# Two block pairs by seven products, and convolution taps moved from VectorE to ScalarE, in a two-layer encoder trunk

## The chip, the cores and the metric

The kernel runs on one core of a Trainium2 chip. The metric is the device time in microseconds (us) of one execution; lower is better. Everything is float32; matrix products use the `float32r` type in a scheme with split operands that is described below.

The engines, with the names of the profile: PE is the matrix engine TensorE (PEld its weight loads), DVE is VectorE, ACT is ScalarE, POOL is GpSimd, SP is the engine that issues most weight loads. Each engine works through its own queue in order, and waits at the head of the queue for semaphores of the others.

## The reference, cut to what matters

Two layers. Each has an attention part (neither changed nor described further here) and a gated feed-forward part with a convolution over positions, width 3:

```
h2 = rms_norm(x, ln2_g[l])                               # (256, 2048)
u  = depthwise_conv(h2 @ w_up[l], conv_w[l], conv_b[l])  # (256, 11264): 3 taps and a bias per column
gate, up = u[..., :5632], u[..., 5632:]
x  = x + (silu(gate) * up) @ w_down[l]                   # back to (256, 2048)
```

## The kernel before

**Tiles.** 256 tokens are two halves of 128 rows. The inner width of 5632 is 44 tiles of 128 (`f` = 0 to 43). The 2048 output columns are four blocks of 512 (`nb` = 0 to 3), and blocks 0 and 1, and blocks 2 and 3, are the two pairs that the change speaks of.

**Split operands.** Every operand of a large product is split into a high part (a copy rounded to `float32r`, written by ACT, `whi` for weights) and the rest (input minus high part, written by DVE, `wlo`). A product is then three: high by high, high by rest, rest by high. The split is in `split` (L114 on ACT, L115 on DVE). So every 1024 columns of weights that PE uses cost one ACT and one DVE instruction of 128x1024 first.

**Quanta and steps.** The work of a layer is a list, `quanta`: each quantum has one weight block of 1 MB (`raw`, three buffers) and a body. A quantum is two or three steps of 1024 weight columns; four steps ahead of PE (`SPLIT_AHEAD`) the split of a step is issued, into five rotating `whi` and five `wlo` buffers. So the high part of a step can only be written once PE is through with the step five before it. Four kinds of quantum matter; the letters are used in the rest of the document:

- U (`q_up`): half of the up projection of one tile `f`; two of them make a tile, which from here on is called one U: 4 steps, 64 products. At its end comes `glu`: add the two parts out of PSUM (`prob`, L548 on ACT and L549 on DVE), scale (`halo`, L550), copy the edge columns (POOL), apply the three taps (L558 on ACT for the middle one; L560 on DVE for the neighbours, two taps by two halves), gate, multiply, split into `mid` tiles. After each odd `f`, `sums_mid` makes four sums for S.
- D (`q_down`): one output block by four tiles of `f`: 2 steps, 24 products with 512 columns.
- S (`q_seven`): a pair of output blocks by two tiles of `f`, by seven products where eight are usual (two token halves, two blocks, two tiles). 6 of the 7 are in S: 3 steps, 18 products of 512 columns. Before the second step DVE forms sums of the weights in `raw` (L755, L756, L757). S over four tile pairs sums up in PSUM; then `add_seven` adds the seven results into `x` (seven additions on DVE, one copy on ACT).
- P (`q_plain`): the seventh product for the eight tiles of a portion: 2 steps, 12 products, and one addition into `x` (L657).

A layer has five portions of `f`: four of 8 tiles and one of 12 (`CHUNKS`). In the first four, blocks 0 and 1 go through S and P, blocks 2 and 3 through D. The order of a portion in steady state: eight U, then P, then S D S D S D S D. The first portion has nine U ahead, so that U is always one tile early.

**Low parts by transfer.** The last step of each U gets its rest not from DVE but from an accumulating DMA (L775 on ACT writes minus the high part into `v_a` or `v_b`, L776 on POOL issues the transfer that adds `raw`).

**What sets the order.** The Tile framework schedules the instructions of each engine ahead of time, by priorities and a model of the times; the queues on the chip then run in that order. `high_priority` around splits moves them forward.

Of the kernel before, what the change touches and what calls it, by code (L numbers as in the profile page):

```python
# [31 lines left out]
NF = FF // P  # L32
# [5 lines left out]
PART = 8  # L38
# [16 lines left out]

SPARE = 3 * (("qT", 3),)

# [4 lines left out]
def encoder_kernel(  # L62
# [107 lines left out]
    def stat_o(grp):  # L170
        ps = psum.tile([P, TT], F32, name="pv", bufs=1)
        for tt in range(TT):
            mm(ps[:, tt:tt + 1], acc_o[grp][:, tt * P:(tt + 1) * P], ones[:, 0:1], True, True)
        st["ro"] = act.tile([P, 16], F32, name="ro", bufs=2)[:, 0:TT]
        rsqrt(ps, 1.0 / (NH * HD), st["ro"], "c2")
# [92 lines left out]
    def evac_qk(ps, nh, kind):  # L268

        n = nh * HD  # L270
        grp, isq = kind[1], kind[0] == "q"
# [246 lines left out]
    gs = {}  # L518
    count = {}

    def middle(l, f):

        name, bufs = "mid", MIDS
        if f >= NF - CHUNKS[-1]:
            k = count[l] = count.get(l, 0) + 1
            if k > MIDS:
                name, bufs = SPARE[k - MIDS - 1]
        return act.tile([P, 2, T], F32R, name=name, bufs=bufs)

# [14 lines left out]
    def glu(l, f, ps):  # L544
# [8 lines left out]
        nc.gpsimd.tensor_copy(ux[:, :, T + r:T + 2 * r - 1], ux[:, :, r + 1:2 * r])  # L553
        y = work.tile([P, 2, T], F32, name="pT", bufs=4)
        for j in range(2):
            c = j * NF + f
            w0, w1, w2, b = (par["conv"][:, l, i, c:c + 1] for i in range(4))
            nc.scalar.activation(y[:, j, :], ux[:, j, r:r + T], AF.Identity, scale=w1, bias=b)  # L558
            for w, o in ((w0, 0), (w2, 2 * r)):
                nc.vector.scalar_tensor_tensor(y[:, j, :], ux[:, j, o:o + T], w, y[:, j, :],  # L560
                                               op0=ALU.mult, op1=ALU.add)
        nc.scalar.activation(t[:, 0, :], y[:, 0, :], AF.Silu)
# [23 lines left out]

    def q_seven(l, c, i):

# [4 lines left out]
        def body(q, part, hi, lo):  # L593
# [20 lines left out]
    def add_seven(ps):  # L614

        t = work.tile([P, 4, HD], F32, name="tq", bufs=2).rearrange("p a d -> p (a d)")
        x11, x12 = x[:, 0, 0:512], x[:, 0, 512:1024]
        x21, x_2, x2_ = x[:, 1, 0:512], x[:, :, 512:1024], x[:, 1, 0:1024].rearrange("p (j n) -> p j n", j=2)
# [22 lines left out]

    def q_plain(l, c):

        f0 = sum(CHUNKS[:c])

        def body(q, half, hi, lo):
# [8 lines left out]
            if half == 1:  # L655
                xv = x[:, 0, 0:512]
                nc.vector.tensor_add(xv, xv, ps)  # L657
        return body

# [42 lines left out]
    for l in range(L):  # L702
# [8 lines left out]
        for c, nf in enumerate(CHUNKS):  # L711
            up = lambda f: [(a["w_up"][l, f, u], q_up(l, f, u), "up") for u in range(2)]
            down = lambda nb, g: [(a["w_down"][l, sum(CHUNKS[:c]) // FG + g, nb], q_down(l, c, nb, g), "")]
            seven = lambda i: [(a["w_seven"][l, c, i], q_seven(l, c, i), "seven")]

            end = sum(CHUNKS[:c]) + PART + 1
            while f < end:
                quanta += up(f)
                f += 1
            quanta.append((a["w_plain"][l, c], q_plain(l, c), ""))  # L720
            if nf == PART:
                for i in range(PAIRS):
                    quanta += seven(i) + down(2 + i // 2, i % 2)
            else:

                for i in range(PAIRS):
# [36 lines left out]
    def by_transfer(s):  # L763
        q, half = steps[s]
        return quanta[q][2] == "up" and half == 1 and last_up[q]

    def low_w(s):

        if s < len(steps) and by_transfer(s):
            q, half = steps[s]  # L770
            src = raw[q][:, half * 1024:(half + 1) * 1024]
            lo = lows[s] = act.tile([P, 1024], F32R, name=("v_a", "v_b")[turns[0] % 2], bufs=1)
            turns[0] += 1
# [137 lines left out]
def _layout(inputs):  # L911
# [33 lines left out]

    four = wd[:, :n * PART * P, :1024].reshape(L, n, PART // 2, 2, P, 2, 512)
    o["w_seven"] = c(np.stack([four[:, :, :, k, :, m] for k, m in ((1, 0), (1, 1), (0, 1), (0, 0))], 4)).reshape(
        L, n, PART // 2, P, 2048)
    o["w_plain"] = c(four[:, :, :, 1, :, 0].transpose(0, 1, 3, 2, 4)).reshape(L, n, P, 2048)
    o["w_down"] = c(f["w_down"].reshape(L, NF // FG, FG, P, NB, 512).transpose(0, 1, 4, 3, 2, 5)).reshape(  # L950
# [40 lines left out]
```

## Time and profile before

| | |
|---|---|
| median of 3 runs | 2098.43 us (2096.87 to 2099.15) |
| the profiled execution | 2098.86 us, span of its instructions 2097.1 us |
| PE busy | 2086.1 us (99%) |
| DVE busy | 1623.0 us (77%) |
| ACT busy | 1308.8 us (62%) |
| POOL busy | 241.5 us (12%) |
| period of one steady portion (8 U, P, 4 S, 4 D) | 129.6 us |
| DVE busy in one such portion | 108.7 us |

A layer is about half of the span; its four portions of eight tiles are eight equal periods in all. The profile's `L` numbers are lines of the kernel before. In the changed kernel the same statements stand some lines lower: `prob` L558, `halo` L559, the multiply by the gate L574, the sums of tiles L587 to L590, the sums of weights L775 to L777, the addition of P L671.

### The profile page before, as it was taken

The page shows a single profiled execution, that of the slowest core. Times are in us where ns is not written, and L with a number is a line of the kernel's source. Part 1 is how long each engine was busy: PE and PEld are TensorE (multiplying, and loading weights), DVE is VectorE, ACT ScalarE, POOL GpSimd, SP SyncE. Part 2 cuts the span into 40 slices and gives each one's busy share as a digit, 9 for nine tenths or more (in the row PEclk, how much of TensorE's full clock was granted, in tenths as well). Part 3 has the DMA queues.
Part 4 walks back from the last instruction along what each step waited for, and adds up shares of the span by engine and source line. Part 5 has one row for each costly group of instructions (what it writes and reads, how often), then busy time and mean ns, then how long its engine had stood idle before and what let it go on. Part 6 is the DMA issues. An engine that isn't in the chain of part 4 may idle for free.

```text
span 2097.1 us, 29473 instructions
## 1 busy us (share of the span) xinstructions
PE 2086.1 (99%) x10816; PEld 1787.8 (85%) x10816; DVE 1623.0 (77%) x2516; ACT 1308.8 (62%) x1905; POOL 241.5 (12%) x325
## 2 busy tenths in 40 slices
PE   9999999999999999999999999999999999999999
PEld 8888888888888888888888888888888888888887
DVE  7786656797887978788857766667978879788786
ACT  7566556766666666576555665567666666666663
POOL 0011101101101011020000111011011110111100
PEclk9999999999999999999999999999999999999999
DMA  9544557858678586787555455578686785867864
GB/s 351 196 145 166 175 181 213 242 204 252 206 253 267 206 258 201 229 272 230 208 181 181 161 169 171 165 220 248 209 256 206 243 254 210 270 199 240 262 211 161
DMA packets 74817, 454.57 MB, mean 217 GB/s; under 512 B 8752, under 2 KB 11312, under 8 KB 26416
## 3 DMA queue, kind: packets, MB, share of 16 engines
q1 hardware_dynamic: 61280, 405.46, 54.4%
q0 software_dynamic: 12672, 46.14, 12.3%
q8 instruction: 85, 1.39, 0.3%
q10 hardware_dynamic: 720, 1.08, 0.2%
q14 instruction: 60, 0.49, 0.1%
HBM read 404.42 MB, written 2.10 MB: 194 GB/s over the span
## 4 chain that ended last, share of the span: by engine, by line
PE 95%; DVE 2%; DMA 1%; issue 1%; ACT 1%; ACTq 0%; DVEq 0%; SPq 0%
PE mm L100 86%; PE S L100 3%; PE pv L100 2%; PE tr L100 1%; DVE wlo L115 1%; PE tr L375 1%; ACT whi L114 1%; PE tr L309 1%; PE S L151 0%; DMA v_a<-raw 0%; DMA mid<-in_xT 0%; DMA raw<-in_w_seven 0%; DMA raw<-in_w_up 0%; DVE pT L560 0%; DVE prob L549 0%
## 5 line engine op out<-in xcount | busy, mean ns | idle before, releaser
L115 DVE TENSOR_TENSOR wlo<-raw,whi 128x1024 fp32r<-128x1024 f32 (+1 forms) x709 | 858.2, 1221 | 298.2 <-ACT whi L114 265.8
L114 ACT ACTIVATE whi<-raw 128x1024 fp32r<-128x1024 f32 (+1 forms) x709 | 736.4, 1053 | 449.9 <-PE mm L100 220.7
L100 PE MATMUL mm<-xs,whi 128*128 128x512 f32 x2816 | 977.0, 390 | 3.0 <-DVE prob L549 3.0
L100 PEld LDWEIGHTS mm<-xs,whi 128*128 128x128 f32 x2816 | 527.8, 188 | 113.9 <-DVE prob L549 3.9
L100 PE MATMUL mm<-xs,wlo 128*128 128x256 f32 x2112 | 596.4, 282 | 0.6 <-DVE wlo L115 0.6
L100 PEld LDWEIGHTS mm<-xs,wlo 128*128 128x128 f32 x2112 | 399.1, 189 | 2.6 <-DVE wlo L115 1.5
L100 PE MATMUL mm<-whi,mid 128*128 128x512 f32 x1412 | 369.9, 392 | 1.6 <-DVE prob L549 1.2
L100 PEld LDWEIGHTS mm<-whi,mid 128*128 128x128 f32 x1412 | 262.5, 188 | 56.6 <-DVE prob L549 2.1
L100 PE MATMUL mm<-whi,xs 128*128 128x512 f32 x1152 | 294.7, 393 | 0.4 <-ACT whi L114 0.4
L100 PEld LDWEIGHTS mm<-whi,xs 128*128 128x128 f32 x1152 | 212.7, 188 | 43.1 <-ACT whi L114 1.4
L100 PE MATMUL mm<-wlo,mid 128*128 128x512 f32 x706 | 201.9, 392 | 0.0
L100 PE MATMUL mm<-wlo,xs 128*128 128x512 f32 x576 | 158.8, 392 | 0.0
L100 PEld LDWEIGHTS mm<-wlo,mid 128*128 128x128 f32 x706 | 132.2, 188 | 27.4
L560 DVE SCALAR_TENSOR_TENSOR pT<-halo,conv,pT 128x256 f32<-128x256 f32 x352 | 148.7, 481 | 6.5 <-ACT pT L558 1.6
L100 PEld LDWEIGHTS mm<-wlo,xs 128*128 128x128 f32 x576 | 107.0, 188 | 21.5
L552 POOL COPY halo<-halo 128x6 f32<-128x6 f32 x88 | 78.4, 891 | 352.8 <-DVE halo L550 352.8
L788 ACT ACTIVATE whi<-raw 128x1024 fp32r<-128x1024 f32 x88 | 92.7, 1053 | 40.1 <-PE mm L100 40.1
L558 ACT ACTIVATE pT<-halo,conv 128x256 f32<-128x256 f32 x176 | 96.0, 592 | 23.2 <-DVE halo L550 21.1
L100 PE MATMUL mm<-xs,v_a 128*128 128x256 f32 x352 | 99.3, 282 | 0.0
L100 PE MATMUL mm<-xs,v_b 128*128 128x256 f32 x352 | 99.2, 282 | 0.0
L776 POOL DMA_DIRECT2D v_b<-raw x44 | 38.1, 866 | 524.1 <-ACT v_b L775 299.6
L549 DVE TENSOR_TENSOR prob<-prob,mm 128x512 f32<-128x512 f32 x88 | 60.3, 685 | 46.9 <-ACT prob L548 46.9
(189 smaller groups left out, 1922.5 us busy)
## 6 DMA issues: line engine op xcount, KB each, us to landing
raw<-in_w_up SPq DMA_DIRECT2D x176, 1024.0 KB, 5.7
raw<-in_w_in SPq DMA_DIRECT2D x71, 1024.0 KB, 4.9
raw<-in_w_down SPq DMA_DIRECT2D x48, 1024.0 KB, 4.9
raw<-in_w_seven SPq DMA_DIRECT2D x40, 1024.0 KB, 5.1
raw<-in_w_out SPq DMA_DIRECT2D x32, 1024.0 KB, 4.8
v_a<-raw POOLq DMA_DIRECT2D x44, 512.0 KB, 5.5
v_b<-raw POOLq DMA_DIRECT2D x44, 512.0 KB, 5.1
raw<-in_w_plain SPq DMA_DIRECT2D x10, 1024.0 KB, 4.9
```

What stands on the lines that cost most here:

```text
L100: nc.tensor.matmul(ps, lhsT, rhs, start=start, stop=stop, skip_group_check=True)
L114: high = nc.scalar.activation(hi, src, AF.Copy)
L115: nc.vector.tensor_sub(lo, src, hi.bitcast(F32))
L309: nc.tensor.transpose(ps[:, j, tt * P:(tt + 1) * P], qn[tt][:, p + j, :], ident)
L375: nc.tensor.transpose(ps[:, kt, tt * P:(tt + 1) * P], p[:, tt, kt * P:(kt + 1) * P], ident)
L549: nc.vector.tensor_add(t, t, ps[:, :, 1])
L552: nc.gpsimd.tensor_copy(ux[:, :, 1:r], ux[:, :, T:T + r - 1])
L558: nc.scalar.activation(y[:, j, :], ux[:, j, r:r + T], AF.Identity, scale=w1, bias=b)
L560: nc.vector.scalar_tensor_tensor(y[:, j, :], ux[:, j, o:o + T], w, y[:, j, :], op0=ALU.mult, op1=ALU.add)
L776: nc.gpsimd.dma_start(out=lo, in_=src, accum_op=ALU.add)
L788: highs[s] = nc.scalar.activation(hl[s][0], raw[q][:, half * 1024:(half + 1) * 1024], AF.Copy)
```

## The change

Four edits.

1. In the first four portions, blocks 2 and 3 go through S and P too (`m` = 1), with their own weights; their D is gone. `add_seven` and P's addition run twice per portion.
2. The order of a portion is now, for each `m`: S, P, S, U, S, U, S, U, U.
3. In `glu` ACT multiplies the neighbour taps (four instructions of 128x256 into two more `pT` tiles) and DVE adds the tiles (two instructions of 128x512), where DVE had four multiply-adds of 128x256.
4. The second step of P gets its rest by transfer, like the last step of U. The tiles for `mid` come from a list of five names with a count of free buffers, since they are kept longer; three tiles change their size by some bytes.

```diff
-        y = work.tile([P, 2, T], F32, name="pT", bufs=4)
+        y, *sides = (work.tile([P, 2, T], F32, name="pT", bufs=4) for _ in range(3))
         for j in range(2):
             ...
             nc.scalar.activation(y[:, j, :], ux[:, j, r:r + T], AF.Identity, scale=w1, bias=b)
-            for w, o in ((w0, 0), (w2, 2 * r)):
-                nc.vector.scalar_tensor_tensor(y[:, j, :], ux[:, j, o:o + T], w, y[:, j, :],
-                                               op0=ALU.mult, op1=ALU.add)
+            for n, w, o in ((sides[0], w0, 0), (sides[1], w2, 2 * r)):
+                nc.scalar.activation(n[:, j, :], ux[:, j, o:o + T], AF.Copy, scale=w)
+        for n in sides:
+            nc.vector.tensor_add(y, y, n)
...
-            if i == PAIRS - 1 and part == 2:
-                with tc.high_priority(offset=AHEAD_PRIO):
-                    add_seven(ps)
+            if part == 2:
+                if m == 1 and i > 0:
+                    drop(l, p)
+                if i == PAIRS - 1:
+                    with tc.high_priority(offset=AHEAD_PRIO):
+                        add_seven(m, ps)
...
-            quanta.append((a["w_plain"][l, c], q_plain(l, c), ""))
             if nf == PART:
-                for i in range(PAIRS):
-                    quanta += seven(i) + down(2 + i // 2, i % 2)
+                for m in range(2):
+                    quanta += seven(0, m) + plain(m)
+                    for i in range(1, PAIRS + 1):
+                        if i < PAIRS:
+                            quanta += seven(i, m)
+                        quanta += up(f)
+                        f += 1
...
     def by_transfer(s):
         q, half = steps[s]
-        return quanta[q][2] == "up" and half == 1 and last_up[q]
+        return half == 1 and (quanta[q][2] == "plain" or last_up.get(q, False))
```

**Where the instructions stand.** Three places. The first is DVE's queue from the last U before P to the splits that follow. Before (second portion; `raw_5097` is the first S, `raw_5137` the first D, `raw_5210` the second S, `mm_5296` holds P's result):

```order
L549 TENSOR_TENSOR prob_5271<-prob_5271,mm_5189 128x512
L115 TENSOR_TENSOR mid_5179<-tq_5174,mid_5179 128x256
L550 TENSOR_TENSOR halo0_110<-prob_5271,acc_b_3144 128x2x256
L115 TENSOR_TENSOR wlo_5291<-raw_5097,whi_5290 128x1024
L657 TENSOR_TENSOR x_70<-x_70,mm_5296 128x512
L115 TENSOR_TENSOR wlo_5304<-raw_5137,whi_5303 128x1024
L115 TENSOR_TENSOR mid_5182<-tq_5174,mid_5182 128x256
L115 TENSOR_TENSOR wlo_5315<-raw_5137,whi_5314 128x1024
```

Now, at the second pair (`m` = 1) of the second portion, the same stretch (`raw_5879` is the second S; the first S and the first step of P have been split ahead of these rows; `mm_6087` holds P's result). First piece:

```order
L558 TENSOR_TENSOR prob_6020<-prob_6020,mm_5935 128x512
L587 TENSOR_TENSOR tq_5920<-bias_5764,bias_5915 128x128
L559 TENSOR_TENSOR halo0_110<-prob_6020,acc_b_3145 128x2x256
L115 TENSOR_TENSOR wlo_6059<-raw_5879,whi_6058 128x1024
L588 TENSOR_TENSOR tq_5920<-tq_5920,bias_5764 128x128
L115 TENSOR_TENSOR mid_5917<-bias_5915,mid_5917 128x256
L775 TENSOR_TENSOR raw_5879<-raw_5879 128x1024
L590 TENSOR_TENSOR tq_5920<-bias_5915,tq_5920 128x128
L571 TENSOR_TENSOR pT_6026<-pT_6026,pT_6027 128x512
L671 TENSOR_TENSOR x_70<-x_70,mm_6087 128x512
```

The rows right behind it, up to the first split of the next U (`raw_5982`):

```order
L776 TENSOR_TENSOR raw_5879<-raw_5879 128x512
L115 TENSOR_TENSOR mid_5925<-tq_5920,mid_5925 128x256
L571 TENSOR_TENSOR pT_6026<-pT_6026,pT_6028 128x512
L115 TENSOR_TENSOR wlo_6069<-raw_5879,whi_6068 128x1024
L115 TENSOR_TENSOR mid_5928<-tq_5920,mid_5928 128x256
L777 TENSOR_TENSOR raw_5879<-raw_5879 128x512
L574 TENSOR_TENSOR bias_6038<-prob_6020,pT_6026 128x256
L589 TENSOR_TENSOR tq_6252<-bias_6038 128x128
L115 TENSOR_TENSOR wlo_6082<-raw_5879,whi_6081 128x1024
L115 TENSOR_TENSOR wlo_6098<-raw_5982,whi_6097 128x1024
```

What moved: the split of the second S and all of `glu` now stand between the last U and the next U with only S, P and S of PE's work beside them, and the addition of P into `x` (L671), which waits for P's last product, stands ahead of the second and third split of the second S. At the first pair (`m` = 0) of most portions L671 stands behind both L571 rows; the rest is alike, with 20 or 21 rows from `prob` to the first split of U (18 in the first portion).

The second place is PE's queue there, from P's last two products (six products of its second step) through the second S (`tr`, `S`, `pv` and `mm_6047` collect its six sums) to the next U (`mm_6144`):

```order
L100 MATMUL mm_6087<-v_a_5952,mid_4973 128x512
L100 MATMUL mm_6087<-v_a_5952,mid_5279 128x512
L100 MATMUL tr_6050<-whi_6058,qtok_4652 128x512 x2
L100 MATMUL mm_6047<-whi_6058,qtok_4490 128x512 x2
L100 MATMUL tr_6050<-wlo_6059,qtok_4652 128x512
L100 MATMUL mm_6047<-wlo_6059,qtok_4490 128x512
L100 MATMUL S_6049<-whi_6068,qtok_4652 128x512 x2
L100 MATMUL S_6048<-whi_6068,qT_4649 128x512 x2
L100 MATMUL S_6049<-wlo_6069,qtok_4652 128x512
L100 MATMUL S_6048<-wlo_6069,qT_4649 128x512
L100 MATMUL pv_6051<-whi_6081,kT_4641 128x512 x2
L100 MATMUL mm_6047<-whi_6081,qT_4649 128x512 x2
```

Behind these rows come the first product of the next U with `whi_6097`, the two products with `wlo_6082`, and the product with `wlo_6098`. Before, the place behind P was held by an S and then by eight products of a D with a high part (`mm_5296<-whi_5303`), ahead of any of its rests.

The third place is ACT's queue at the end of the last U, first before and then now (`whi_6043` is the second step of P):

```order
L562 ACTIVATE prob_5155<-pT_5161 128x256
L114 ACTIVATE mid_5171<-bias_5169 128x256
L114 ACTIVATE whi_5248<-raw_5097 128x1024
L548 ACTIVATE prob_5271<-mm_5189 128x512
L114 ACTIVATE mid_5179<-tq_5174 128x256
```

```order
L572 ACTIVATE prob_5897<-pT_5903 128x256
L809 ACTIVATE whi_6043<-raw_5839 128x1024
L557 ACTIVATE prob_6020<-mm_5935 128x512
L114 ACTIVATE whi_6058<-raw_5879 128x1024
L114 ACTIVATE mid_5917<-bias_5915 128x256
```

What moved: a 128x1024 high part, which waits for the same U, now stands ahead of the copy of U's result.

More of the change, by code (lines that the diff above doesn't have):

```diff
@@ L54 @@
 WARM = 14
-SPARE = 3 * (("qT", 3),)
+MIDDLE = (("mid", MIDS), ("qT", 3), ("qtok", 3), ("kT", 2), ("kTb", 1))
 EARLY = 7
@@ L173, in stat_o @@
             mm(ps[:, tt:tt + 1], acc_o[grp][:, tt * P:(tt + 1) * P], ones[:, 0:1], True, True)
-        st["ro"] = act.tile([P, 16], F32, name="ro", bufs=2)[:, 0:TT]
+        st["ro"] = act.tile([P, TT], F32, name="ro", bufs=2)
         rsqrt(ps, 1.0 / (NH * HD), st["ro"], "c2")
@@ L268, in evac_qk @@
     def evac_qk(ps, nh, kind):
+        if "pad" not in par:
+            par["pad"] = work.tile([P, 8], F32, name="pad", bufs=1)
         n = nh * HD
@@ L518, in encoder_kernel, with drop @@
     gs = {}
-    count = {}
+    free, kept = {}, {}
     def middle(l, f):
[L523 to L528, printed above, removed]
+        if f == 0 and l not in kept:
+            free.clear()
+            free.update(MIDDLE)
+            kept[l] = {}
+        name = max(free, key=lambda n: (free[n] > 0, n == "mid", free[n]))
+        assert free[name] > 0
+        free[name] -= 1
+        kept[l].setdefault(f // 2, []).append(name)
+        return (work if name == "qtok" else act).tile([P, 2, T], F32R, name=name, bufs=dict(MIDDLE)[name])
+    def drop(l, p):
+        for name in kept[l].pop(p):
+            free[name] += 1
     def q_up(l, f, u):
@@ L771, in low_w @@
             src = raw[q][:, half * 1024:(half + 1) * 1024]
-            lo = lows[s] = act.tile([P, 1024], F32R, name=("v_a", "v_b")[turns[0] % 2], bufs=1)
+            n = turns[0] % 2
+            lo = lows[s] = act.tile([P, 1024 + 8 * n], F32R, name=("v_a", "v_b")[n], bufs=1)[:, 0:1024]
             turns[0] += 1
```

30 lines of the change are left out of this document (17 added, 13 removed).

## The prediction

> **What bounds the kernel now.** I read the page first, then what PE waits for, then one steady portion by windows. The page's head and its chain of waits:
>
> ```profile
> span 2097.1 us, 29473 instructions
> PE 2086.1 (99%) x10816; PEld 1787.8 (85%) x10816; DVE 1623.0 (77%) x2516; ACT 1308.8 (62%) x1905; POOL 241.5 (12%) x325
> PE 95%; DVE 2%; DMA 1%; issue 1%; ACT 1%; ACTq 0%; DVEq 0%; SPq 0%
> ```
>
> Of PE's waits over the whole span, us in total, times, longest:
>
> ```profile
> PE mm L100 <- DVE prob L549: 4.3, 4, 1.7
> PE mm L100 <- DVE wlo L115: 0.6, 2, 0.4
> ```
>
> PE is the bound and never starves: some 5 us in 2097. So time can be won only by fewer products, and lost only where PE begins to wait. How near is that? Stretches of one steady portion (busy us and, behind x, the instructions of PE, PEld, DVE, ACT, POOL), the whole portion last:
>
> ```profile
> 436.90:448.00 11.10, 11.10 (x50) 9.19 (x50) 11.07 (x16) 5.70 (x8) 0.00 (x0) 1.00 0.53 180
> 448.00:460.00 12.00, 12.00 (x55) 9.93 (x54) 11.86 (x12) 4.97 (x5) 0.00 (x0) 1.00 0.67 259
> 460.00:480.00 20.00, 20.00 (x102) 17.03 (x101) 18.67 (x22) 13.99 (x15) 1.72 (x2) 1.00 0.69 230
> 566.50:696.10 129.60, 129.60 (x693) 112.45 (x693) 108.70 (x158) 84.07 (x111) 16.53 (x24) 1.00 0.74 236
> ```
>
> In the 43 us of S and D, DVE is busy 41.6 us (97%) while PE loses nothing; in the portion as a whole it is 108.7 of 129.6 us. There DVE lives on the start that it has from the eight U. The change takes out D, where DVE does least, and adds S, where it does most.
>
> **Prices.** PE at the end of the last U, and eight products with 512 columns in a row; then DVE at the same place, where it is saturated, so that the distance of two starts is the price of an instruction:
>
> ```profile
> 430.03 0.28 PE L100 MATMUL mm<-xs,v_a 128*128 128x256 f32 x1
> 446.03 1.98 PE L100 MATMUL mm<-whi,mid 128*128 128x512 f32 x8
> ```
>
> ```profile
> 427.31 1.22 DVE L755 TENSOR_TENSOR raw<-raw 128x1024 f32<-128x1024 f32 x1
> 428.44 0.28 DVE L577 TENSOR_TENSOR tq<-bias 128x128 f32<-128x128 f32 x1
> 428.64 0.42 DVE L115 TENSOR_TENSOR mid<-bias,mid 128x256 fp32r<-128x256 f32 x1
> 428.98 0.69 DVE L756 TENSOR_TENSOR raw<-raw 128x512 f32<-128x512 f32 x1
> 429.58 0.28 DVE L578 TENSOR_TENSOR tq<-tq,bias 128x128 f32<-128x128 f32 x1
> 429.78 1.22 DVE L115 TENSOR_TENSOR wlo<-raw,whi 128x1024 fp32r<-128x1024 f32 x1
> 430.92 0.69 DVE L757 TENSOR_TENSOR raw<-raw 128x512 f32<-128x512 f32 x1
> 431.52 0.29 DVE L580 TENSOR_TENSOR tq<-bias,tq 128x128 f32<-128x128 f32 x1
> 431.72 0.68 DVE L549 TENSOR_TENSOR prob<-prob,mm 128x512 f32<-128x512 f32 x1
> 432.32 0.42 DVE L115 TENSOR_TENSOR mid<-tq,mid 128x256 fp32r<-128x256 f32 x1
> 432.65 0.69 DVE L550 TENSOR_TENSOR halo<-prob,acc_b 128x512 f32<-128x512 f32 x1
> 433.26 1.22 DVE L115 TENSOR_TENSOR wlo<-raw,whi 128x1024 fp32r<-128x1024 f32 x1
> 434.39 0.69 DVE L657 TENSOR_TENSOR x<-x,mm 128x512 f32<-128x512 f32 x1
> 434.99 1.22 DVE L115 TENSOR_TENSOR wlo<-raw,whi 128x1024 fp32r<-128x1024 f32 x1
> 436.12 0.42 DVE L115 TENSOR_TENSOR mid<-tq,mid 128x256 fp32r<-128x256 f32 x1
> 436.46 1.22 DVE L115 TENSOR_TENSOR wlo<-raw,whi 128x1024 fp32r<-128x1024 f32 x1
> 437.60 0.88 DVE L560 SCALAR_TENSOR_TENSOR pT<-halo,conv,pT 128x256 f32<-128x256 f32 x2
> 438.39 1.23 DVE L115 TENSOR_TENSOR wlo<-raw,whi 128x1024 fp32r<-128x1024 f32 x1
> ```
>
> One product is (1.98 - 0.39) / 7 = 0.227 us (0.39: the last one's own length). On DVE: 1024 columns 1.14, 512 columns 0.60, 256 columns 0.34, 128 columns 0.20, and a multiply-add of 256 columns 0.79 / 2 = 0.40. The end of an instruction comes 0.09 after its price (1.22 against 1.14). For ACT, with DVE's row that one of them waits for:
>
> ```profile
> 430.41 0.60 ACT L548 ACTIVATE prob<-mm 128x512 f32<-128x512 f32 x1 [0.71 <-PE mm L100]
> 431.70 2.01 ACT L114 ACTIVATE whi<-raw 128x1024 fp32r<-128x1024 f32 x2 [0.38 <-DVE raw L757]
> 422.94 1.08 ACT L558 ACTIVATE pT<-halo,conv 128x256 f32<-128x256 f32 x2
> 442.51 0.69 DVE L757 TENSOR_TENSOR raw<-raw 128x512 f32<-128x512 f32 x1
> 443.32 3.91 ACT L114 ACTIVATE whi<-raw 128x1024 fp32r<-128x1024 f32 x4 [0.32 <-DVE raw L757]
> ```
>
> A high part costs 0.95 (3.91 less one length of 1.05, by three), a tap about 0.5, the copy of U's result ends 0.9 after PE's last issue slot of U (430.15, 0.12 behind the last start; then 430.41 plus 0.60). From the end of L757 to a high part that waits for it are 0.1 us.
>
> **What PE saves.** Per portion D goes (4 x 24 = 96 products) and S and P come (72 + 12): 12 products less, 2.7 us. Two layers, four portions: 96 products, **21.8 us**. A steady portion then has 126.9 us of PE's work.
>
> **What DVE does in a portion.** By these prices: a U 3 x 1.14 + 2 x 0.60 (`prob`, `halo`) + 2 x 0.60 (the taps; before 4 x 0.40) + 2 x 0.34 + half of `sums_mid` 0.74 = 7.2; an S 3 x 1.14 + 1.14 + 1.20 = 5.8; a P 1.74; `add_seven` 5.9. Eight U, eight S, two P, two `add_seven`: 119 of 126.9 us (94%); the same sum for before gives some 104. The move of the taps frees only 0.4 us per U, since DVE still adds. ACT gets some 32 x 0.5 + 8 = 24 us on top of 84.1: it stays below 110 and waits for others rather than they for it. The transfers and loads that the change adds, with the median us from issue to landing in the last column:
>
> ```profile
> raw<-in_w_seven SPq DMA_DIRECT2D x40, 1024.0 KB, 5.1
> v_a<-raw POOLq DMA_DIRECT2D x44, 512.0 KB, 5.5
> ```
>
> Two more transfers per portion (10 for 8) are issued seven steps ahead of their use; even if all seven were steps of S (six products) that is 7 x 1.36 = 9.5 us for a landing of 5.5. One more load in 26 finds a DMA share of 0.74 in the portion. I cost both at nothing; with that cover gone a transfer would cost PE its landing, 16 times 5.5 us.
>
> **What happens at S, P, S.** 94% on average leaves room, but not here. Let t = 0 be PE's start on the first S after the last U. Ahead of it DVE can have at most four steps: the high part of the fifth needs a buffer of a step that PE is just through with. So S and the first step of P are ready (5.5 us of PE). PE wants the second S from 30 products on, t = 6.8, and the first rest of the next U after 48 products and one more: **t = 11.1**.
>
> DVE's queue up to that rest is in the order above. `prob` cannot start before ACT's copy: 0.9; now a high part stands before it, 0.95 more: 1.8. From `prob` to that split the prices add up to 10.9, and the split itself needs 1.14 + 0.09: DVE delivers at 1.8 + 10.9 + 1.2 = 13.9 if it never waits, 2.8 us late. It does wait, twice. At the second pair L671 stands behind nine rows from `prob` on (5.0 us, t = 6.8) and waits for P's last product, seen at 6.8 + 0.26 = 7.1. The ten rows from L671 on and the split behind them take 5.9 + 1.2, so t = 14.2. And the high part of the third step waits for L777, which ends at 7.1 + 0.60 x 4 + 0.34 x 2 + 1.14 + 0.09 = 11.4; ACT 0.1 + 1.05 later, 12.5, while DVE had the row ready at 11.8. Two splits are left, 2 x 1.14 + 0.09. That makes **t = 14.9, 3.8 us late**. At the first pair L671 comes too late in the queue to wait; L777 costs about 0.25: 14.2, 3.1 late; in the first portion of a layer two rows are missing, 2.7. PE's wait falls in three pieces, ahead of the second and third step of S and the first rest of U, each below 2 us; it is not made up, since PE has no slack. Behind it nothing else is queued that matters: U's 11.1 us let DVE catch up (it needs 7.2), the next `prob` is in time by about 0.7 us for the PSUM tile that the U after next takes, and `add_seven` has two U to lie beside.
>
> Per span: 8 second pairs x 3.8 + 6 first pairs x 3.1 + 2 x 2.7 = **54.4 us**. Bounds: from below, DVE starts `prob` at 0.9 and waits only for P: 13.0 at the first pairs (1.9 late), 14.2 at the second (3.1): 40 us. From above, DVE comes to t = 0 with part of `add_seven` (5.9) undone, and misses the PSUM tile: 1.3 more (the 0.7, and one row of `add_seven`, 0.6) at each of 16: 75 us. I take 54.4: the rows fix the order, and a saturated DVE in the trace follows its prices exactly.
>
> **Sum**: 2098.9 - 21.8 + 54.4 = 2131.5, said as **2131 us**; by the bounds 2117 to 2152. The profiled execution is 0.4 us above the median of the runs, which changes nothing.
>
> **The rivals.**
>
> *All hidden* (faster): DVE's 119 of 126.9 us fit, PE waits nowhere: 2077. For it speaks that DVE ran at 97% for 43 us with no wait of PE. Against it: there each S was followed by a D, 5.5 us of PE for 2.3 of DVE. [...]
>
> *One place of two*: only the second pairs pay, through L671, 8 x 3.1 = 25 us, and the first pairs hide theirs: 2102, about the same. For it: L671 is the one wait that the first pairs lack. Against it: their 10.9 us of rows do not shrink.
>
> *A backlog* (slower still): DVE does not get four steps ahead in the two U with `add_seven`, and each S, P, S begins late; from 1.5 us more at each place, above 2155. For it: 22 us of PE there for about 20 of DVE. Against it: the second U alone returns 3.9.
>
> **How the numbers follow.** The forecast 0.69, *all hidden* 0.17, *one place* 0.06, *backlog* 0.08. The forecast's own range is 2110 to 2152; with part of the others 2088 to 2155 leaves out *all hidden* and little else. A measurement of this kernel tells about 0.2% (4 us) from no change: faster 0.17, within 0.06, slower 0.77.
>
> **What would show it.** Right: PE waits for `wlo` and `whi` some 3 us per half portion, in three pieces around the second S, and DVE waits for PE at L671 in second pairs; PE's count falls by 96; the U, S, U, S stretch has no wait. Wrong: no PE wait at S, P, S, which would mean that DVE reached `prob` with more than four steps done or its rows cost less; or waits at the head of U for `prob`, which would be the backlog.

## The result

The changed kernel takes **2196.33 us** (median of 3 runs, 2194.92 to 2204.13) where the kernel before takes 2098.43: 1.0478 of its time, 95% interval 1.0439 to 1.0517. It is slower by 98 us; the prediction said 33 slower, and its range ended at 2155. The head of the page, the shares of the chain of waits, and span and clock of the core, after the change:

```profile
span 2194.4 us, 29580 instructions
PE 2109.5 (96%) x10720; PEld 1783.2 (81%) x10720; DVE 1728.7 (79%) x2522; ACT 1503.8 (69%) x2331; POOL 239.5 (11%) x343
PE 64%; DMA 14%; DVE 11%; ACT 7%; issue 4%; POOL 0%; ACTq 0%; SPq 0%; DVEq 0%
core 0: 2194.4 us, clock 0.986
```

The same row of the kernel before:

```profile
core 0: 2097.1 us, clock 1.000
```

Three things are to be seen. PE has 96 products less, yet is busy for 23 us more. PE's idle time grew from 11 us (2097.1 - 2086.1) to 85. And the clock that was granted to PE, 1.000 before, is 0.986. The waits of PE (us in total, times, longest):

```profile
PE mm L100 <- DVE prob L558: 30.8, 22, 3.1
PE S L100 <- DVE wlo L115: 20.8, 16, 1.7
PE pv L100 <- ACT whi L114: 18.3, 16, 1.4
PE S L100 <- ACT whi L114: 3.2, 6, 0.7
PE mm L100 <- DVE x L671: 2.7, 2, 1.6
PE mm L100 <- DVE wlo L115: 2.4, 6, 0.4
```

Rows two, three, four and six are the second S and the first rest of the next U, 44.7 us; the first row is 30.8 us where it was 4.3. Of these, 25.6 are at the head of a U, which waits for `prob` to free its PSUM tile, 1.2 at the start of P, and 4.0 (two waits) in the last portions, of 12 tiles.

**One place S, P, S.** The second pair of the first portion, PE's timeline (start, duration, in brackets the idle time and its releaser): the start of the first S, the first rest of the second S, its third step, the first rest of the next U. Behind it two rows of DVE there:

```profile
497.81 0.62 PE L100 MATMUL tr<-whi,mid 128*128 128x512 f32 x2
508.25 0.73 PE L100 MATMUL S<-wlo,mid 128*128 128x512 f32 x2 [1.18 <-DVE wlo L115]
510.34 0.74 PE L100 MATMUL pv<-whi,mid 128*128 128x512 f32 x2 [1.35 <-ACT whi L114]
512.73 0.39 PE L100 MATMUL mm<-xs,wlo 128*128 128x256 f32 x1 [0.40 <-DVE wlo L115]
```

```profile
499.64 0.69 DVE L558 TENSOR_TENSOR prob<-prob,mm 128x512 f32<-128x512 f32 x1
504.83 0.69 DVE L671 TENSOR_TENSOR x<-x,mm 128x512 f32<-128x512 f32 x1
```

From 497.81 to 512.73 are 14.92 us; without waits they would be 11.1. `prob` starts at t = 1.83. The prediction had t = 14.9 and 1.8.

**The clock.** Most later places are worse. Stretches at the third place (us, then busy us and, behind x, the instructions of PE, PEld, DVE, ACT, POOL; then the granted clock, the DMA share, GB/s):

```profile
573.59:577.00 3.41, 1.72 (x7) 0.75 (x5) 3.41 (x6) 2.50 (x4) 0.01 (x1) 1.00 0.13 50
577.00:580.41 3.41, 2.70 (x6) 1.70 (x7) 3.19 (x7) 2.59 (x3) 0.85 (x1) 0.50 0.64 124
580.41:583.83 3.42, 3.42 (x11) 2.84 (x10) 3.42 (x4) 2.56 (x4) 0.00 (x0) 0.50 0.88 281
```

At 577.0 the clock is halved, for 6.8 us, and the products of that time take nearly twice as long: at 580.80 to 581.65 those of 512 columns start 0.42 to 0.43 us apart, at 572.80 to 573.48 0.22 to 0.23. The trace's record of the clock has 14 such spells in the span, of 3.4 or 6.8 us, 61.4 us together; before there was none. No wait at this place was longer than 1.5 us. Ten of the spells begin at S, P, S; the other four begin behind one wait for `prob` of 2.6 to 3.1 us.

**The balance.** The rows of PE's timeline give the lateness of each of the 16 places, as above (time from the start of S to U's first rest, less 11.1). Where no half clock falls into it, it is 3.1 to 3.3 us at first pairs and 3.8 at second pairs. At these values (eight second pairs, six first pairs, two first portions: 8 x 3.82 + 6 x 3.3 + 2 x 3.1) 16 places make some 56.6 us; measured with the half clock they make 72.5. So 97.3 us more span = 21.8 saved, against 56.6 at S, P, S, about 28 for the half clock (an estimate: PE is busy in 56.6 of its 61.4 us, by chance the same number, and half of that would have done at full clock), 26.5 more of waits for `prob`, and 3.6 for two smaller waits (`x` 2.7, `mid` 0.9); about 4 are left. Products around a wait take longer (two of them 0.73 us behind a wait at 508.25, 0.62 at 497.81), which may be a part of that; it is not worked out.

### The profile page after: what moved, and what is told of

Its sections match the earlier page's. It is cut to its first block, busy times and chain, and to the rows that moved or that the text cites. A ratio compares the mean times of both kernels' runs of the same rounds, so it can differ in the third digit from the quotient of the medians.

```text
span 2194.4 us, 29580 instructions
## 1 busy us (share of the span) xinstructions
PE 2109.5 (96%) x10720; PEld 1783.2 (81%) x10720; DVE 1728.7 (79%) x2522; ACT 1503.8 (69%) x2331; POOL 239.5 (11%) x343
## 3 DMA queue, kind: packets, MB, share of 16 engines
q10 hardware_dynamic: 720, 1.08, 0.2%
## 4 chain that ended last, share of the span: by engine, by line
PE 64%; DMA 14%; DVE 11%; ACT 7%; issue 4%; POOL 0%; ACTq 0%; SPq 0%; DVEq 0%
PE mm L100 58%; DMA raw<-in_w_up 6%; DVE wlo L115 5%; DMA raw<-in_w_seven 4%; ACT whi L114 4%; PE S L100 2%; PE pv L100 2%; DMA v_b<-raw 2%; DMA v_a<-raw 1%; DVE raw L775 1%; ACT pT L569 1%; PE tr L100 1%; DVE pT L571 1%; DVE prob L558 1%; DVE raw L777 1%
## 5 line engine op out<-in xcount | busy, mean ns | idle before, releaser
L115 DVE TENSOR_TENSOR wlo<-raw,whi 128x1024 fp32r<-128x1024 f32 (+1 forms) x739 | 893.5, 1219 | 317.5 <-ACT whi L114 287.9
L114 ACT ACTIVATE whi<-raw 128x1024 fp32r<-128x1024 f32 (+1 forms) x739 | 769.1, 1053 | 430.8 <-PE mm L100 202.9
L100 PE MATMUL mm<-xs,whi 128*128 128x512 f32 x2816 | 994.6, 395 | 28.3 <-DVE prob L558 25.6
L100 PE MATMUL mm<-whi,mid 128*128 128x512 f32 x1024 | 286.5, 396 | 6.6 <-DVE prob L558 5.2
L100 PEld LDWEIGHTS mm<-whi,mid 128*128 128x128 f32 x1024 | 191.2, 189 | 49.5 <-DVE prob L558 7.3
L569 ACT ACTIVATE pT<-halo,conv 128x256 f32<-128x256 f32 x352 | 150.0, 497 | 4.4 <-POOL halo L561 2.0
L100 PE MATMUL mm<-wlo,mid 128*128 128x512 f32 x476 | 148.5, 395 | 0.0
L571 DVE TENSOR_TENSOR pT<-pT 128x512 f32<-128x512 f32 x176 | 120.9, 687 | 27.1 <-ACT pT L569 22.6
L809 ACT ACTIVATE whi<-raw 128x1024 fp32r<-128x1024 f32 x106 | 111.4, 1051 | 10.4 <-PE mm L100 8.9
L100 PEld LDWEIGHTS mm<-wlo,mid 128*128 128x128 f32 x476 | 89.8, 189 | 18.4
L567 ACT ACTIVATE pT<-halo,conv 128x256 f32<-128x256 f32 x176 | 95.6, 590 | 10.1 <-DVE halo L559 9.6
L797 POOL DMA_DIRECT2D v_a<-raw x53 | 46.2, 871 | 498.1 <-ACT v_a L796 273.9
```

What stands on the lines that cost most here:

```text
L100: nc.tensor.matmul(ps, lhsT, rhs, start=start, stop=stop, skip_group_check=True)
L114: high = nc.scalar.activation(hi, src, AF.Copy)
L115: nc.vector.tensor_sub(lo, src, hi.bitcast(F32))
L569: nc.scalar.activation(n[:, j, :], ux[:, j, o:o + T], AF.Copy, scale=w)
L571: nc.vector.tensor_add(y, y, n)
L797: nc.gpsimd.dma_start(out=lo, in_=src, accum_op=ALU.add)
```

## The experiments

Two theories at first. **Place** (theory 1 where an expectation says so): S, P, S ask more of DVE and ACT than PE's work there covers, and what else is slow follows from PE's idling there; elsewhere DVE has room. **Full queue**: DVE's rows and its own waits fill the whole period, so a wait that is removed comes back at another place. Every kernel below is the changed one with the edit named, unless it says otherwise. What they gave, in us; the fourth column is PE's waits for `wlo` and `whi`, and "half clock" is from the trace's record (spells that end within the span). In the kernels that have S, P, S, the waits for `wlo` and `whi` lie there, but for 3.6 us in e_fill, 6.7 in e_taps_back, 5.8 in e_no_sums_1 and at most 1 us in the others. The change was run three times, e_order four times, the other experiments once; the three runs of the change spread over 9 us, so a difference of less than some 10 us says nothing.

| run | time | PE busy | waits for `wlo`, `whi` | waits for `prob` | half clock |
|---|---|---|---|---|---|
| before | 2098.4 | 2086.1 | 1.0 | 4.3 | 0 |
| the change | 2196.3 | 2109.5 | 44.7 | 30.8 | 61.4 |
| e_order | 2221.8 | 2117.8 | 52.3 | 22.5 | 47.8 |
| e_fill | 2176.3 | 2131.5 | 13.4 | 16.1 | 17.1 |
| e_plain_dve | 2228.2 | 2122.1 | 55.2 | 37.5 | 92.2 |
| e_taps_back | 2210.7 | 2116.0 | 58.5 | 28.7 | 99.0 |
| e_before_taps | 2117.0 | 2093.3 | 9.3 | 2.9 | 3.4 |
| e_pool_adds | 2196.3 | 2119.4 | 52.7 | 6.8 | 102.4 |
| e_no_sums_23 | 2148.9 | 2095.2 | 38.5 | 3.7 | 41.0 |
| e_no_sums_1 | 2157.2 | 2099.5 | 7.3 | 22.4 | 61.4 |
| e_no_sums_123 | 2131.2 | 2084.8 | 0.2 | 26.3 | 30.7 |
| e_no_sums_taps | 2116.5 | 2075.2 | 1.5 | 16.6 | 6.8 |
| e_order_no_sums | 2162.9 | 2094.7 | 40.5 | 1.1 | 34.1 |
| e_half_up | 2179.9 | 2110.2 | 48.5 | 10.0 | 68.3 |
| e_half_all | 2103.2 | 2071.8 | 1.3 | 5.5 | 10.2 |

**e_order: the same work in another order.** Each pair as P, S, U, S, U, S, U, S, U, so that only P and the first S stand together (with it, a pair's `mid` tiles are given free at S and not at P).

```diff
...
-                    quanta += seven(0, m) + plain(m)
-                    for i in range(1, PAIRS + 1):
-                        if i < PAIRS:
-                            quanta += seven(i, m)
-                        quanta += up(f)
+                    quanta += plain(m)
+                    for i in range(PAIRS):
+                        quanta += seven(i, m) + up(f)
```

> Only the order of a portion differs from the change: for each pair P, S, U, S, U, S, U, S, U, so that no two S stand with only P between them (a pair's first tiles are given free at S, not at P). All products, splits and transfers are the same in number. Theory 1 (the loss is made at S, P, S: 45 us of PE's waits there, and the low clock and the late loads that follow from them): PE's waits at the second S are gone, the granted clock is 1.00, the time is 2077 to 2095. Rival (DVE is simply too full with 94% of a portion, wherever S stands): the waits only move, the time stays above 2150.

Measured 2221.81 (4 runs, 2219.31 to 2224.62), 1.0591 of before (1.0570 to 1.0612): slower than the change itself. PE's waits, largest first:

```profile
PE mm L100 <- DVE wlo L115: 47.2, 34, 1.8
PE mm L100 <- DVE prob L558: 22.5, 27, 1.3
PE mm L100 <- DVE tq L636: 9.6, 12, 1.2
PE tr L100 <- DVE x L638: 9.1, 16, 0.6
```

The waits have moved: the first row is now 34 waits for a rest in P, S and U, and the next pair waits for `add_seven` (L636, L638), which now has a U and P beside it where it had two U. The place theory in its simple form falls.

**e_fill: PE is given work at the place.** Twelve products that nobody reads, in the second S of each pair: 192 more, 43.6 us.

```diff
+            if c < 4 and i == 1 and part > 0:
+                for _ in range(6):
+                    mm(cur["dn"][:, 1], xs[0][:, 0, 0:P], xs[1].rearrange("p a t -> p (a t)"), True, True)
```

> The change, with twelve products (2.7 us) that nobody reads put into PE's queue at the second S of each pair, into the unused half of P's PSUM tile, where PE waits for the rests. Theory 1 says that PE's idle time there lets the granted clock fall to a half for 3.4 or 6.8 us, 14 times and 61 us in all in the change, which costs about 30 us: with the gap filled the clock stays at 1.00, and the time falls to 2160 to 2175 although PE does 192 products more. Rival (the clock falls for another cause, or its fall costs nothing, since PE waits for DVE then anyhow): the time stays at 2190 or rises by up to 40.

2176.27, just above the 2160 to 2175 expected: with 43.6 us more of work the kernel is 20 us faster. The waits for `wlo` and `whi` at S, P, S fall to 9.8, those for `prob` to 16.1, and the half clock from 14 spells (61.4 us) to 3 (17.1 us). PE's busy time grows by 22.0 us only (2131.5 - 2109.5) for 43.6 us of products; the 21.6 that are missing are about half of the 44.3 us of half clock that are gone. That the clock fell in the change because PE idled is shown by this.

**e_plain_dve: P's second rest from DVE again** (the transfer of edit 4 undone; 18 transfers less).

```diff
-        return half == 1 and (quanta[q][2] == "plain" or last_up.get(q, False))
+        return half == 1 and last_up.get(q, False)
```

> The change, but the second step of P gets its rest from DVE again (88 transfers instead of 106). Theory 1 with late loads as the cause of the 31 us that PE waits at the head of U for the last U's sum: the transfers hold the weight buffers and the loads queue behind them, so these waits fall below 15 us; DVE has one split more at S, P, S, 1.1 us at 16 places: 18 us more there, the time 2185 to 2200. Rival (the heads of U wait since DVE and ACT are late by themselves): the waits at the head of U stay at 30 us or more, the time rises to 2210 or more.

2228.18, 32 us slower, and the waits for `prob` go up to 37.5 instead of down. So the added transfers are not what makes the heads late by themselves; 18 more rows of DVE cost more than they.

**e_taps_back: the taps on DVE, as before** (edit 3 undone), and **e_before_taps: the kernel before with edit 3 alone.** The edit is the one shown in the diff of the change.

> The change, but the neighbour taps are multiplied and added by DVE as before (four instructions of 128x256), and ACT has only the middle tap. Theory 1: DVE has 0.4 us more per U, so S, P, S waits some 0.4 us longer at 16 places, 6 us; the time is 2190 to 2210. Rival (the longer chain through ACT, six taps instead of two, is what makes the sum of U late): the waits at the head of U go, the time falls to 2160 or below.

> The kernel before with the third edit alone: the neighbour taps multiplied by ACT, added by DVE. All theories of the loss expect no change: PE does not wait there, DVE gets 0.4 us less per U, ACT 2 us more: 2094 to 2102. If the longer chain through ACT costs by itself, the time rises by 5 us or more and PE waits at the head of U.

2210.66, and 2117.0 beside 2096.87 of the kernel before. So moving the taps gains 14 us in the changed kernel and costs 20 us in the one before, where no change was expected (2094 to 2102). There DVE had room, and what grew was ACT's queue. PE's longest waits in e_before_taps:

```profile
PE pv L100 <- ACT whi L114: 6.0, 8, 1.0
PE S L100 <- ACT whi L114: 3.3, 5, 1.2
PE mm L100 <- DVE prob L549: 2.9, 4, 1.6
```

The first two name ACT, and are 0.4 us before; ACT is busy for 1442.7 of 2115.2 us (68%). Four more instructions of 0.50 us for each U stand in a queue that also writes every high part; a high part behind them is late though ACT has idle time.

**e_pool_adds: the additions of the taps' tiles on POOL.**

```diff
-            nc.vector.tensor_add(y, y, n)
+            nc.gpsimd.tensor_add(y, y, n)
```

> The change, with the two additions of the tap tiles done by POOL instead of DVE, which takes 1.2 us per U from DVE, 4.8 us per half portion. After the order experiment two theories stand. Full queue: DVE with its waits for ACT fills the whole period (61.4 us busy and 7 us of waits in 70), so each us taken from it anywhere comes back: 16 x 4.8 = 77 us, and the clock's 30: 2090 to 2125. Place: only what stands at S, P, S counts, 1.2 us there: 16 x 1.2 = 19 us, 2165 to 2180. A loss is possible if POOL's additions take so long that the sum of U is late: above 2200.

2196.3, no change, outside all that was expected, and that hides two large ones: the waits for `prob` fall to 6.8 and those for `wlo` at the second S double to 41.5. DVE has 176 rows less but is busy for 1725.6 us (1728.7 in the change). Its groups of additions in `raw`, first in the change and then here, and POOL's (busy, mean ns):

```profile
L776 DVE TENSOR_TENSOR raw<-raw 128x512 f32<-128x512 f32 x72 | 49.3, 685 | 0.5
```

```profile
L571 POOL TENSOR_TENSOR pT<-pT 128x512 f32<-128x512 f32 x176 | 265.6, 1509 | 124.2 <-ACT pT L569 117.3
L776 DVE TENSOR_TENSOR raw<-raw 128x512 f32<-128x512 f32 x72 | 77.5, 1076 | 1.4
```

The same DVE instruction took 0.69 us alone and 1.66 while POOL added (at two places of this run: 437.62 beside POOL, 452.70 with POOL idle):

```profile
436.52 3.91 POOL L571 TENSOR_TENSOR pT<-pT 128x512 f32<-128x512 f32 x2 [0.69 <-ACT pT L569]
437.62 1.66 DVE L776 TENSOR_TENSOR raw<-raw 128x512 f32<-128x512 f32 x1
...
452.70 0.69 DVE L776 TENSOR_TENSOR raw<-raw 128x512 f32<-128x512 f32 x1
```

**e_no_sums_1 and e_no_sums_23: DVE's work is taken away.** L775 to L777 are left out, in the second S alone, or in the third and fourth (the S concerned multiply unsummed weights).

```diff
-        if part == 1:
+        if part == 1 and sums:
```

> The change with work left out: the three sums of weights on DVE are not formed for the second S of each pair, the one behind P: 2.3 us of DVE per half portion, at the place of the waits. Place: the waits there fall from 45 to below 10 us and the clock stays high, 2100 to 2130. Full queue: half of what leaving out two S elsewhere gives, 16 x 2.3 = 37 us, 2150 to 2165.

> The change with work left out: the three sums of weights on DVE are not formed for the third and fourth S of each pair (the raw weights are split instead), 4.7 us of DVE per half portion, all of it outside of S, P, S. Full queue: 16 x 4.7 = 75 us and the clock, 2090 to 2125. Place: the waits at the second S stay (45 us), only the heads of U gain: 2165 to 2195.

2157.24 and 2148.93. Each takes away one kind of wait and leaves the other. Without the sums of the second S, only 1.5 us of waits for `wlo` and `whi` are left at S, P, S (5.8 more are two waits in the last portions), but `prob` keeps 22.4 and PE waits 12.7 us for the transfers; without the others, away from S, P, S, `prob` falls to 3.7 and S, P, S keep 38.5. The 16 places there are late by 60.0 us together, 3.1 to 4.5 each. So neither theory alone: the place has its own price, near the predicted one, and the heads of U have another.

**e_no_sums_123 and e_no_sums_taps: both at once**, the second with the taps on DVE again. **e_order_no_sums** has the order of e_order without these sums. The line that says which S do without, against e_no_sums_1:

```diff
-                                           sums=quanta[q][1].place not in (1,))
+                                           sums=quanta[q][1].place not in (1, 2, 3))
```

> The changed kernel without the weight sums (three instructions of VectorE, 2.34 us) of the second, third and fourth S of each pair in the first four portions: those S multiply unsummed weights, and their share of the output is not the reference's. The two kernels that left out one part of these sums gained 39 us (second S: its waits went, those at the heads of U stayed) and 47 us (third and fourth: the reverse). Theory 1 (both kinds of wait come from one queue, VectorE's, that is full over the portion, and from the transfers and loads that slip behind it): with both left out both kinds go, waits for prob below 6 us, for wlo and whi at the second S below 12 us (what the longer queue of ScalarE leaves), and the lowered clock nearly gone; 2085 to 2110 us, no less than the sum of the two gains. Theory 2 (the waits at the heads of U have a cause of their own in the loads, which VectorE only shifts): 2120 us or more, with waits for prob or for the weight buffers above 15 us.

> As the kernel without the weight sums of the second, third and fourth S (those S multiply unsummed weights), and the neighbour taps are applied by VectorE again as before. On the kernel before, the taps on ScalarE alone cost 20 us. Theory 1 (ScalarE's longer chain in glu delays the high parts by itself, whatever VectorE does): the kernel without sums is 5 to 20 us slower than this one, waits for ACT whi fall to below 3 us here, and this one comes to 2077 to 2092 us, the time of its products. Theory 2 (with a VectorE that has room the taps cost nothing on ScalarE): the two within 4 us of each other, or this one the slower.

> The order P, S, U, S, U, S, U, S, U for each pair (2221.8 us with all sums), and the weight sums of the second, third and fourth S left out (those S multiply unsummed weights). Theory 1 (that order failed because VectorE's queue has no room, wherever the work is put): without the sums it falls by 80 us or more, to 2085 to 2140, and its waits for wlo (47.2 us) to below 15 us. Theory 2 (the order itself is bad: add_seven stands in the way of the next pair's S and P): it stays above 2160 us, and waits for x and tq of add_seven stay near their 18.7 us.

2131.20, 2116.45, 2162.88. The gains do not add up (39 + 47 = 86 expected, 65 measured): S, P, S are in time to 0.8 us at every place, DVE's busy time (1616.2 us) is that of the kernel before, and yet `prob` is waited for nearly as much as in the change. PE's waits in e_no_sums_123:

```profile
PE mm L100 <- DVE prob L558: 26.3, 12, 3.5
PE mm L100 <- DVE x L672: 4.9, 7, 1.6
PE mm L100 <- DMA v_a<-raw: 2.9, 4, 1.0
PE mm L100 <- DMA v_b<-raw: 2.8, 4, 1.1
```

And the chain of waits that ends in one of them (start, us, what):

```profile
636.45 7.93 DMA raw<-in_w_up
...
645.40 4.78 DMA raw<-in_w_up
...
651.23 1.05 ACT whi L114
...
652.30 0.55 DVE wlo L115
...
653.45 0.69 DVE prob L558
...
654.18 0.89 PE mm L100 x3
```

`prob` has its input, but in DVE's queue a split stands ahead of it, that split waits for ACT's high part, and that for a load of U's weights that came late. All 12 waits for `prob` in this kernel lead back over such a load of U's weights. With the taps on DVE this kernel gains 15 us (but comes to 2116, not to the 2077 to 2092 expected): here, with room on DVE, ACT's longer queue is the dearer one, as in e_before_taps. The order of e_order falls by 59 us without the sums, and is still 32 us slower than e_no_sums_123: its waits for `add_seven` (18.3 us for `x` L640) and for `wlo` (38.4) are its own. Full queue was not its only trouble.

**e_half_up and e_half_all: the loads are shortened.** U loads half of each weight block and multiplies it twice; e_half_all does it in e_no_sums_taps.

```diff
-            m = 2048 // parts
+            m = (1024 if quanta[q][2] == "up" and q > 2 else 2048) // parts
...
+    def part_of(q, half):
+        half = 0 if quanta[q][2] == "up" and q > 2 else half
+        return raw[q][:, half * 1024:(half + 1) * 1024]
```

> The changed kernel with U loading only the first half of each weight block (512 KB for 1 MB), and multiplying that half twice: U's output is not the reference's. The work of TensorE, VectorE and ScalarE is the same instruction by instruction; only the loads are shorter. Theory 1 (the waits at the heads of U are the loads and the accumulating transfers, late behind each other where S, P and S free their buffers close together): waits for prob fall from 30.8 us to below 10, those of the second S stay (35 to 55 us), and the time falls by 20 to 40 us, to 2155 to 2177. Theory 2 (the heads wait for VectorE's full queue and the loads only look late): prob stays above 20 us, 2185 us or more.

> As the kernel without the weight sums of the second, third and fourth S and with the taps on VectorE again (2116.5 us; waits for prob 16.6 us, for P's addition x 15.1 us), and U loads half of each weight block and multiplies it twice (neither U nor those S have the reference's output). Theory 1 (what is left there is late loads): waits for prob below 4 us; those for x, P's addition behind the whole of glu in VectorE's queue, stay 8 to 16 us, and the time is 2090 to 2105 us. If x goes as well, 2077 to 2088, the time of the products alone. Theory 2 (loads play no part): 2112 us or more.

2179.85 and 2103.23. PE's waits in e_half_up, and further down the loads with their landing:

```profile
PE S L100 <- ACT whi L114: 30.3, 16, 2.6
...
PE mm L100 <- DVE prob L558: 10.0, 16, 1.1
```

One of the waits of the second row, in PE's timeline, 5.4 us behind the start of a first S, so at the first product of P:

```profile
502.87 1.20 PE L100 MATMUL mm<-whi,mid 128*128 128x512 f32 x4 [1.10 <-DVE prob L558]
```

```profile
raw<-in_w_up SPq DMA_DIRECT2D x176, 512.0 KB, 3.9
v_a<-raw POOLq DMA_DIRECT2D x53, 512.0 KB, 4.6
```

With the loads short, `prob` falls from 30.8 to 10.0 us, and 9.2 of these are waits at P, inside S, P, S; at the heads of U 0.8 us are left of 25.6. In e_half_all, `prob` falls from 16.6 to 5.5. So what is loaded late causes nearly all of the waits at the heads in the change, and two thirds of them in e_no_sums_taps. (The transfers land sooner as well, `v_a` in 4.6 us for 6.6, so that the two are not told apart by this.) The time falls by 16 us only (20 to 40 expected). The 16 places S, P, S are now late by 96.1 us together (72.5 in the change), the 9.2 at P among them, with the half clock at 68.3. The order of single rows differs a little between these two kernels, so this is not shown to be a rule; but e_pool_adds does the same (heads and P 6.8, places 93.2 us), and it is what a full queue would do. Where DVE has room, in e_half_all, the rest is PE's wait for P's addition, 16.9 us for `x` L671 in six times, which stands behind `glu` in DVE's queue.

No run beat the kernel before. The best, 2103.2, leaves out work and is 26 us above the 2077 of the products alone.

## Why the prediction was wrong, point by point

- **What PE saves**: right. 10816 products became 10720; in e_half_all, with little idle time, PE is busy for 14.3 us less than before; of the 7.5 that are missing to 21.8, half clock explains about 5 (10.2 / 2).
- **S, P, S**: right in place, pieces and size. Three pieces, longest 1.7 us. `prob` at t = 1.83, U's first rest at 14.92 (1.8 and 14.9 predicted), 3.8 late at second pairs, as said. First pairs are 3.3 late for 3.1, first portions 3.1 and 3.2 for 2.7. The sum at these values is 56.6 for 54.4. One wait was smaller than said, without harm: in second pairs L671 waits for P for 0.1 us at most, not 0.3; it starts at t = 7.02, as P's last product ends. Taking the sums away (e_no_sums_123) takes this term away but for 4.8 us, which shows it.
- **The term that was missing: the clock**. The working had each wait "below 2 us" and stopped there, at the price of the idle time itself; the clock was put at nothing without a reason. But at ten places PE's clock was halved beside such waits, two or three within 6 us, and at four more behind one wait for `prob` of 2.6 to 3.1 us; some 28 us by the estimate above, of them 16 within S, P, S (72.5 - 56.6). The profile of before does not show it, as PE hardly idles there; the page has a row for the granted clock, and a term with PE idle in bursts needs a rival for it.
- **The step that failed: transfers and loads "at nothing"**, and with it "the next `prob` is in time by about 0.7 us". The waits for `prob` are 26.5 us more than before. I compared landing times of before (5.5 and 5.1) with the time between issue and use, and gave a price only for the transfer itself. In the change the median landing of `v_a` is 6.6 us, of `in_w_plain` 7.0 (before 4.9). S, P and S use 3 MB of weights in 10.9 us of PE's work, and free three buffers close together. One head of U, followed back:

```profile
734.45 10.16 DMA v_b<-raw
...
744.75 5.09 DMA raw<-in_w_up
...
749.92 0.07 ACT v_a L796
...
752.85 0.95 ACT whi L114
753.79 0.48 ACT prob L557
754.27 0.96 ACT whi L114
755.23 0.68 DVE prob L558
...
755.95 0.61 PE mm L100 x2
```

  The transfer reads `raw`, so its buffer is free only when it has landed, here after 10.16 us; the next load waits for that buffer; the copy into `v_a` waits for the load at the head of ACT's queue, and behind it stand the high parts and the copy of U's result. A margin of 0.7 us at that PSUM tile does not hold against it. I asked what the transfer delays, and not what holds the buffer that it reads. This is one of the ways in which a load comes late: of the 17 waits for `prob` over 0.5 us, 15 lead back over a load of U's weights, and ahead of the load stands a transfer of 6.0 to 10.2 us in 7 of them, a row of ACT or DVE in 8. e_half_up, with short loads, has 0.8 us left at the heads; e_plain_dve shows that it is not only the 18 added transfers, since without them the waits for `prob` are longer still.
- **"ACT waits for others rather than they for it"**: wrong, and so was the taps' move at no cost. ACT's busy time came as predicted (51.6 us in the half portion below, 103 in a portion). But edit 3 alone costs the kernel before 20 us, with ACT at 68%. Four more rows in an in-order queue, between a high part's input and the high part, were a delay there at that share. In the changed kernel the edit still gains 14 us, as DVE is shorter of time there.
- **DVE's sum**: 119 us predicted for a portion, and for the kernel before the same sum gave 104, where the profile has 108.7. One half portion of the change, from one second S to the next, by the columns of the stretches above:

```profile
440.27:508.25 67.98, 64.72 (x340) 54.71 (x340) 60.98 (x82) 51.59 (x76) 8.27 (x13) 1.00 0.76 240
```

  That is 122 us in a portion. In the same stretch DVE waits 5.7 us for ACT's high parts and 0.9 for its taps; with 61.0 busy that is 67.6 of 68.0 us, where PE's products alone would take 63.5 (126.9 / 2). DVE's queue is full there, and "U's 11.1 us let DVE catch up" was too kind.
- **The rivals**: *all hidden* and *one place of two* are excluded by the rows at S, P, S. The *backlog*, above 2155, has the right end, but its mechanism was `add_seven`. The waits for `prob` came, mostly through loads.
- **What stays open**: how far the heads and S, P, S trade with each other. Three runs (e_pool_adds, e_half_up, e_order) show that relieving one raises the other; only the leaving out of DVE's sums, and e_fill, which gives PE more to do, lower both.

## What to carry to other kernels

Price an idle burst of PE twice: for the time itself, and for the clock, which in the change stood at half for 61.4 us beside 85 us of idle time, some 28 us by the estimate above. When an edit uses up loaded weights faster at one place, follow the buffer and not the landing: who still reads it, which load waits for it, and what stands behind that load's first reader in an in-order queue. And an engine that is busy for 68% may delay PE where the rows that PE needs stand behind new ones, as ACT did in e_before_taps (20 us); do such a move alone on the old kernel before it is counted as free.

## What the runs showed of the hardware

**Where the clock was halved.** In the change the 14 spells are ten of 3.41 us and four of 6.83. In the 3.41 us ahead of each of them PE was busy for 0.88 to 1.72 us, as in the stretch at 573.59, shown above (1.72). Two stretches with waits at S, P, S, and no halving behind them:

```profile
508.74:512.15 3.41, 2.06 (x9) 1.16 (x7) 2.85 (x5) 2.92 (x4) 0.10 (x1) 1.00 0.81 154
788.65:792.06 3.41, 2.01 (x7) 1.18 (x8) 2.94 (x6) 3.40 (x5) 0.86 (x1) 1.00 0.29 58
```

The kernel before has a stretch of 3.41 us with 1.66 us of PE's work (985.01 to 988.42), and its clock is 1.00 there and in the stretch behind it. In the change a wait of 2.85 us for `prob` at 753.1 was followed by no halving, one of 2.66 at 1634.6 was. So neither the busy time of such a stretch nor the length of a wait tells by itself whether a halving follows, and what else decides it is not shown by these runs.

**What half clock costs**: in e_fill PE's busy time is 21.6 us below what the added products would give, for 44.3 us less of half clock, 0.49 us for each us (with fewer waits as well). Among kernels with the same 10720 products PE's busy time grows with it, 2075.2 us at 6.8 of half clock (e_no_sums_taps), 2109.5 at 61.4, 2122.1 at 92.2 (e_plain_dve): 0.55 us for each us, from the first and the last. That holds other things too, since e_no_sums_1 and the change have the same 61.4 and are 10 us apart.

**POOL's addition** of 128x512 takes 1.51 us on average (e_pool_adds, beside other work) where DVE takes 0.69 alone, and a DVE addition beside it took 1.66 in the row shown; the mean of L776 is 1.08 us there and 0.69 in the change.
